# A pad behind the constants and one in the last stage: new byte places for the matmul operands of a hybrid S5 and pooling layer

## The chip, the cores and the metric

One core of one Trainium2 chip runs the whole kernel as one program. The metric is the device time of one execution in microseconds (us). Engines are named as in the profile: PE (matmuls), PEld (PE's weight loads, which run beside matmuls), DVE, ACT and POOL (elementwise work), SP (issues most DMAs).

## The reference, cut to what matters

One layer on `x` of shape (1, 2048, 1024), all in float32:

```python
h = rmsnorm(x, norm_g)
proj = h @ w_in + b_in                       # 1024 x 4096: ua, za, ub, zb (512 each), ga, gb (1024 each)
ya = s5_branch(ua, ...) * silu(za)           # diagonal complex state space, then a 512 x 512 GLU
yb = pool_branch(ub, pool_w, pool_scale) * silu(zb)
merged = sigmoid(ga) * (ya @ w_branch_a) + sigmoid(gb) * (yb @ w_branch_b)
x = x + merged @ w_out
return rmsnorm(x, final_norm_g)
```

## The kernel before, in words

**Matmuls.** Every large product is made from operands split into a high and a low part (`split`, L92 to 99), both kept as float32r tiles. `mm3` (L101 to 104) then issues three matmuls: the high weights against the high moving part (L102), the high weights against the low moving part (L103), the low weights against the high moving part (L104). In most stages the weights are 128 by 128 and the moving operand has 512 columns. Each matmul of the program brings its own weight load, so in a row of matmuls the weights of the next one are loaded while this one streams. "A group of three" below is one call of `mm3`.

**Stages, in the order of PE's work.** The sequence is cut into four chunks of 512 columns, and `hT0` to `hT3` hold the normalised, transposed input, 8 row blocks each.

- *Projections.* `proj_block` (L592) makes one block of 128 output channels for one chunk from 8 groups of three, moving operand `hT`, weights `wt` (or, for two of the four UA blocks, `w_first2` and `w_first3` from pool `d1`, which are kept for the whole UA stage, L189). The stages are UA, ZA (beside it `matrices`, which builds the state-space matrices on DVE and POOL, L424), UB and ZB with the pooling, and GA and GB. Beside the GA and GB blocks runs `scan` (L659), a generator that is advanced by one step per block: for each of 8 units it goes through `run_in`, `run_scan`, `table`, `run_taps`, the split of `sp` into `spl` (L830) and `run_out`, with matmuls of 256 columns.
- *GLU* (L1067 to 1086): moving operand `yhl`, weights `wg`, 64 groups of three.
- *Branches and output* (L1144 to 1196): for each chunk 64 groups with `yab` against `wt`, then 64 with `wo` against `mt`; the last row tile of the last chunk is cut into two halves of 256 columns.

**Order of the work.** The program is recorded in the order in which the code runs, for each engine one queue. `pump` (L131) splits the next weight tile and issues the load of one further on. Pools are opened and closed by stage. A tile that is laid over bytes of an earlier one waits for that one's last use, so where a tile lies decides what its first writer waits for.

**Places.** Pools `const`, `raw`, `w`, `stg`, `par` and the pools of the stages (`d1` to `d6`, `fin`) are laid one behind the other from the low end of a partition's memory. `hT`, `xp` and `big` (which holds `wo` and `yab`) are laid from the high end. The first pool is `const`:

```python
    RD = const.tile([128, G // 2], F32, name="RD")
    PH = const.tile([128, 2, G // 2], F32, name="PH")
```

Of the kernel before, what the change touches and what calls it, by code (L numbers as in the profile page):

```python
# [9 lines left out]
F32 = mybir.dt.float32  # L10
F32R = mybir.dt.float32r
# [25 lines left out]
def hybrid_kernel(ctx: ExitStack, tc: tile.TileContext, x, norm_g, w_in, b_in, log_dt, lam_re, lam_im,  # L37
# [9 lines left out]
    const = ctx.enter_context(tc.tile_pool(name="const", bufs=1))  # L47
# [7 lines left out]
    def sub(stack, name, side="left"):  # L55
        return stack.enter_context(tc.tile_pool(name=name, bufs=1, side=side, reuse_waits="tile"))
# [21 lines left out]
    rcnt = const.tile([128, 16], F32, name="rcnt")  # L78
    RD = const.tile([128, G // 2], F32, name="RD")
    PH = const.tile([128, 2, G // 2], F32, name="PH")  # L80

    def bcol(n):
        return cols[:, n:n + 1]
# [42 lines left out]
    hl = {}  # L126
# [58 lines left out]
    idn = par.tile([128, 128], F32, name="idn")  # L185
    s_d = ExitStack()
    d1 = sub(s_d, "d1")

    def w_first(key):  # L189
        t = d1.tile([128, 2, 1024], F32R, name=f"w_first{key[1]}")  # L190
        hl[key] = t
        return t[:, 0, :], t[:, 1, :], lambda r: r

    UA, ZA, UB, ZB, GA, GB = 0, 4, 8, 12, 16, 24
# [4 lines left out]
    for n in range(NB):  # L199
        w_in_job(n, plain if n < 2 else w_first)  # L200
# [10 lines left out]
    def ts(o, i, s1, o0, s2=None, o1=None):  # L211
        if s2 is None:
            V.tensor_scalar(out=o, in0=i, scalar1=s1, scalar2=None, op0=o0)
        else:
            V.tensor_scalar(out=o, in0=i, scalar1=s1, scalar2=s2, op0=o0, op1=o1)
# [6 lines left out]
    def pieces(v, bits, count):  # L222

        import struct
        if (v, bits, count) not in kept:
            res, left = [], v
            for _ in range(count - 1):
                m, e = math.frexp(left)
                q = math.ldexp(math.floor(m * 2 ** bits), e - bits)
                res.append(q)  # L230
                left -= q
            res.append(struct.unpack("f", struct.pack("f", left))[0])
            kept[v, bits, count] = res
        return kept[v, bits, count]
# [67 lines left out]
    def params(d, V, ldt, lam, dn):  # L302
# [61 lines left out]
        for h in range(2):  # L364
            r = slice(h * 64, (h + 1) * 64)
            V.tensor_copy(out=PH[r, 0], in_=ang[r, h::2])
        a0, a1, pn = PH[:, 0], PH[:, 1], d.tile([128, H], F32, name="pn")
        turn = pieces(64 * math.pi, 11, 4)
# [290 lines left out]
    def scan(d):  # L659
# [53 lines left out]
        def phases():  # L713
# [4 lines left out]
            for j in range(LV):  # L718
                ts(th[:, j], PH[:, 1], float(T << j), ALU.mult)
                ts(lo[:, j], PH[:, 0], float(T << j), ALU.mult)  # L720
            ts(n, th, 2.0 / math.pi, ALU.mult, MAGIC, ALU.add)
# [174 lines left out]
    for i in reversed(range(NB)):  # L896
# [23 lines left out]
        for k in range(2):  # L920
            n = min(T, win - 1 - k * T)
# [145 lines left out]
    for c in range(NCH):  # L1067
        t = yhl[c]
# [23 lines left out]
    d6 = sub(s_d, "d6")  # L1092
# [4 lines left out]
    def load_gate(c, n):  # L1097
        t = d6.tile([128, 2, 512], F32, tag="gt", bufs=3, name="gt")
        SP.dma_start(out=t, in_=Gd[n][c].rearrange("b p k -> p b k"))
        gts[c, n] = t  # L1100
# [22 lines left out]
    def finish(tt):  # L1123
# [12 lines left out]
            A.dma_start(out=outr[tt // 2, k0:k0 + 128, cs], in_=r[:, cs])  # L1136
        x2.pop(tt)

    load_gate(0, 0)
    load_gate(0, 1)  # L1140
    gb = d6.tile([128, D], F32, name="gb")
# [82 lines left out]
```

## Time and profile before

| | |
|---|---|
| median of 3 runs | 1236.32 us (1235.59 to 1238.8) |
| the profiled execution | 1238.27 us, of which the span of the profile 1236.4 us |
| PE busy | 1205.5 us (97% of the span), 5413 matmuls |
| weight loads busy | 975.1 us (79%) |
| DVE, ACT, POOL busy | 730.8, 395.3, 346.4 us |
| mean granted clock of TensorE | 0.993 of full |

The profile starts at the first instruction. The time of an execution is longer than the span by what lies around it, here 1.87 us. A matmul's duration in the profile reaches to a modelled end, and neighbours overlap; how fast PE goes is read from one matmul's start to the next one's.

### The profile page before, as it was taken

The page shows a single profiled execution, that of the slowest core. Times are in us where ns is not written, and L with a number is a line of the kernel's source. Part 1 is how long each engine was busy: PE and PEld are TensorE (multiplying, and loading weights), DVE is VectorE, ACT ScalarE, POOL GpSimd, SP SyncE. Part 2 cuts the span into 40 slices and gives each one's busy share as a digit, 9 for nine tenths or more (in the row PEclk, how much of TensorE's full clock was granted, in tenths as well). Part 3 has the DMA queues.
Part 4 walks back from the last instruction along what each step waited for, and adds up shares of the span by engine and source line. Part 5 has one row for each costly group of instructions (what it writes and reads, how often), then busy time and mean ns, then how long its engine had stood idle before and what let it go on. Part 6 is the DMA issues. An engine that isn't in the chain of part 4 may idle for free. (4 is left out here: it accounts for less than half of the span.)

```text
span 1236.4 us, 14778 instructions
## 1 busy us (share of the span) xinstructions
PE 1205.5 (97%) x5413; PEld 975.1 (79%) x5413; DVE 730.8 (59%) x1310; ACT 395.3 (32%) x622; POOL 346.4 (28%) x232
## 2 busy tenths in 40 slices
PE   6999989999999999999999999999999999999996
PEld 5887867788888888888888888887878888888885
DVE  5586378153543668777788773046565855755615
ACT  6542211222222232443333432244333322322202
POOL 3321167011110212332334321234562312213312
PEclk9999989999999999999999999999999999999998
DMA  8413233201111232433334332178766553563502
GB/s 295 133 43 84 58 112 126 80 17 54 43 45 43 83 110 88 129 91 110 113 94 128 96 102 78 66 227 253 247 218 209 182 188 131 175 207 105 188 1 102
DMA packets 149783, 149.94 MB, mean 121 GB/s; under 512 B 23584, under 2 KB 111184, under 8 KB 149712
## 3 DMA queue, kind: packets, MB, share of 16 engines
q1 hardware_dynamic: 127424, 112.28, 30.6%
q10 hardware_dynamic: 22288, 36.73, 7.9%
q8 instruction: 42, 0.69, 0.2%
q14 instruction: 29, 0.24, 0.1%
HBM read 99.43 MB, written 49.55 MB: 120 GB/s over the span
## 5 line engine op out<-in xcount | busy, mean ns | idle before, releaser
L102 PE MATMUL mm<-hT,wt 128*128 128x512 f32 x960 | 382.5, 398 | 0.0
L103 PE MATMUL mm<-hT,wt 128*128 128x512 f32 x960 | 380.6, 396 | 0.0
L104 PE MATMUL mm<-hT,wt 128*128 128x512 f32 x960 | 379.9, 396 | 0.0
L104 PEld LDWEIGHTS mm<-hT,wt 128*128 128x128 f32 x960 | 180.8, 188 | 44.1
L103 PEld LDWEIGHTS mm<-hT,wt 128*128 128x128 f32 x960 | 181.1, 189 | 43.5 <-DVE hT L98 0.9
L102 PEld LDWEIGHTS mm<-hT,wt 128*128 128x128 f32 x960 | 181.2, 189 | 42.7
L96 POOL TENSOR_TENSOR wt<-raw,wt 128x1024 fp32r<-128x1024 f32 x30 | 85.5, 2849 | 316.5 <-ACT wt L94 316.5
L1027 ACT ACTIVATE go<-mm,half 128x512 f32<-128x512 f32 x64 | 43.9, 686 | 204.9 <-PE mm L104 190.2
L102 PE MATMUL mm<-yab,wt 128*128 128x512 f32 x256 | 101.2, 395 | 1.8 <-DVE gt L1160 1.8
L104 PE MATMUL mm<-yab,wt 128*128 128x512 f32 x256 | 101.0, 395 | 0.0
L103 PE MATMUL mm<-yab,wt 128*128 128x512 f32 x256 | 101.0, 395 | 0.0
L94 ACT ACTIVATE wt<-raw 128x1024 fp32r<-128x1024 f32 x62 | 65.5, 1057 | 60.7 <-PE mm L104 34.2
L1162 POOL TENSOR_TENSOR m<-gt 128x512 f32<-128x512 f32 x32 | 52.1, 1630 | 100.4 <-DVE gt L1160 71.6
L1121 POOL TENSOR_TENSOR r<-r,gb 128x512 f32<-128x512 f32 (+1 forms) x33 | 41.1, 1260 | 138.4 <-ACT xt L1118 138.3
L96 DVE TENSOR_TENSOR wt<-raw,wt 128x1024 fp32r<-128x1024 f32 x32 | 58.6, 1831 | 19.7 <-ACT wt L94 19.6
L845 ACT ACTIVATE st<-mm,half 128x512 f32<-128x512 f32 x32 | 22.1, 690 | 145.9 <-PE mm L104 114.5
L1160 DVE SCALAR_TENSOR_TENSOR gt<-gt,mm 128x512 f32<-128x512 f32 x64 | 42.3, 680 | 32.8 <-PE mm L104 27.9
L102 PEld LDWEIGHTS mm<-yab,wt 128*128 128x128 f32 x256 | 48.0, 187 | 14.4 <-issue 2.6
L104 PEld LDWEIGHTS mm<-yab,wt 128*128 128x128 f32 x256 | 48.0, 187 | 11.7
L103 PEld LDWEIGHTS mm<-yab,wt 128*128 128x128 f32 x256 | 48.0, 187 | 11.6
L104 PE MATMUL mm<-wo,mt 128*128 128x512 f32 (+1 forms) x136 | 52.0, 383 | 0.0
L103 PE MATMUL mm<-wo,mt 128*128 128x512 f32 (+1 forms) x136 | 52.0, 382 | 0.0
(272 smaller groups left out, 1920.3 us busy)
## 6 DMA issues: line engine op xcount, KB each, us to landing
xt<-in_x SPq DMA_DIRECT2D x32, 512.0 KB, 5.4
raw<-in_w_in SPq DMA_DIRECT2D x32, 512.0 KB, 4.4
Gd<-go ACTq DMA_DIRECT2D x64, 256.0 KB, 2.4
gt<-Gd SPq DMA_DIRECT2D x32, 512.0 KB, 4.8
raw<-in_w_branch_a SPq DMA_DIRECT2D x32, 256.0 KB, 3.1
raw<-in_w_branch_b SPq DMA_DIRECT2D x32, 256.0 KB, 3.5
out<-r ACTq DMA_DIRECT2D x32, 256.0 KB, 2.3
Ud<-uo ACTq DMA_DIRECT2D x16, 256.0 KB, 2.1
```

Of the source, the lines that this page charges most:

```text
L94: A.activation(hi, src, AF.Copy, scale=1.0 if scale is None else scale)
L96: (eng or V).tensor_tensor(out=lo, in0=src, in1=hi.bitcast(F32), op=ALU.subtract)
L102: PE.matmul(ps, lhsT=sh, rhs=mh, start=first, stop=False)
L103: PE.matmul(ps, lhsT=sh, rhs=ml, start=False, stop=False)
L104: PE.matmul(ps, lhsT=sl, rhs=mh, start=False, stop=last)
L845: A.activation(t, ps, AF.Tanh, bias=hcol(n), scale=0.5)
L1027: A.activation(o, ps, AF.Tanh, bias=hcol(n), scale=0.5)
L1121: GP.tensor_tensor(out=r, in0=r, in1=gb[:, cs], op=ALU.mult)
L1160: V.scalar_tensor_tensor(out=gt[:, b], in0=gt[:, b], scalar=1.0, in1=pss[b], op0=ALU.add, op1=ALU.mult)
L1162: GP.tensor_tensor(out=m, in0=gt[:, 0], in1=gt[:, 1], op=ALU.add)
```

## The change

A tile of 48 floats (192 bytes per partition) that nothing uses is added at the end of `const`, and one of 32 floats (128 bytes) as the first tile of `d6`. The two `w_first` tiles are allocated when `d1` is opened, ahead of all its other tiles. No instruction is added, removed or moved on any engine.

```diff
@@ -78,6 +78,7 @@
     rcnt = const.tile([128, 16], F32, name="rcnt")
     RD = const.tile([128, G // 2], F32, name="RD")
     PH = const.tile([128, 2, G // 2], F32, name="PH")
+    const.tile([128, 48], F32, name="lpad")
 
     def bcol(n):
         return cols[:, n:n + 1]
@@ -185,10 +186,10 @@
     idn = par.tile([128, 128], F32, name="idn")
     s_d = ExitStack()
     d1 = sub(s_d, "d1")
+    firsts = {n: d1.tile([128, 2, 1024], F32R, name=f"w_first{n}") for n in (2, 3)}
 
     def w_first(key):
-        t = d1.tile([128, 2, 1024], F32R, name=f"w_first{key[1]}")
-        hl[key] = t
+        t = hl[key] = firsts[key[1]]
         return t[:, 0, :], t[:, 1, :], lambda r: r
 
     UA, ZA, UB, ZB, GA, GB = 0, 4, 8, 12, 16, 24
@@ -1136,6 +1137,7 @@
             A.dma_start(out=outr[tt // 2, k0:k0 + 128, cs], in_=r[:, cs])
         x2.pop(tt)
 
+    d6.tile([128, 32], F32, name="pad6")
     load_gate(0, 0)
     load_gate(0, 1)
     gb = d6.tile([128, D], F32, name="gb")
```

What this does to the places, as the allocator gives them (start of the operand, in bytes modulo 512; every slice of these tiles that a matmul reads starts a multiple of 512 bytes further on):

| moving operand, weights | columns | groups of three | before: moving / weights | now: moving / weights |
|---|---|---|---|---|
| `hT`, `wt` | 512 | 960 | 480 / 288 | 480 / 480 |
| `hT`, `w_first2`, `w_first3` | 512 | 64 | 480 / 192 and 256 | 480 / 32 |
| `yab`, `wt` | 512 | 256 | 480 / 288 | 480 / 480 |
| `wo`, `mt` | 512 | 248 | 480 / 160 | 480 / 480 |
| `wo`, `mt` | 256 | 16 | 480 / 160 | 480 / 480 |
| `yhl`, `wg` | 512 | 64 | 288 / 288 | 480 / 480 |
| `plhl`, `pw` (pooling) | 512 | 16 | 384 / 384 | 64 / 64 |
| `uu`, `bt`; `uu`, `mz`; `spl`, `ca` (scan) | 256 | 96 | 288 / 288 | 480 / 480 |

Some tiles lie over other bytes than before, so a few first writers wait for something else. The queue of SP at the loads of `matrices` is one such place (`cn`, and `B_1320` and `B_1321`, now `B_1321` and `B_1322`, hold the matrices C and B in pool `d2`). Before:

```order
L427 DMA cn<-in_ssm_c_re 128x4x64 [waits DMAHW1_49,PE_49]
L427 DMA cn<-in_ssm_c_im 128x4x64 [waits DMAHW3_49]
L427 DMA cn<-in_ssm_c_re 128x4x64 [waits DMAHW4_49]
L431 DMA B_1320<-in_ssm_b_re 64x32x16 [waits DMAHW5_49]
L432 DMA B_1320<-in_ssm_b_im 64x32x16 [waits DMAHW6_49]
```

The same place on SP's queue in the changed kernel:

```order
L428 DMA cn<-in_ssm_c_re 128x4x64 [waits DMAHW1_49,PE_49]
L428 DMA cn<-in_ssm_c_im 128x4x64 [waits DMAHW3_49]
L428 DMA cn<-in_ssm_c_re 128x4x64 [waits DMAHW4_49]
L432 DMA B_1321<-in_ssm_b_re 64x32x16 [waits DMAHW5_49,PE_49]
L433 DMA B_1321<-in_ssm_b_im 64x32x16 [waits DMAHW6_49]
```

The order is the same; the first load of B now also waits for PE, since it is laid over `w_first3`, whose last matmul ends the UA stage.

## Rows read from the trace of the kernel before

**Rows 1.** The page: PE's busy time, share and instructions; its granted clock in 40 slices.
```profile
PE 1205.5 (97%) x5413; PEld 975.1 (79%) x5413; DVE 730.8 (59%) x1310; ACT 395.3 (32%) x622; POOL 346.4 (28%) x232
...
PEclk9999989999999999999999999999999999999998
```

**Rows 2.** Groups by form on PE: shapes, xcount | busy us, mean ns | idle before.
```profile
L102 PE MATMUL mm<-hT,wt 128*128 128x512 f32 x960 | 382.5, 398 | 0.0
...
L102 PE MATMUL mm<-yab,wt 128*128 128x512 f32 x256 | 101.2, 395 | 1.8 <-DVE gt L1160 1.8
...
L102 PE MATMUL pso<-wo,mt 128*128 128x512 f32 x128 | 50.6, 395 | 0.0
...
L102 PE MATMUL mm<-wo,mt 128*128 128x512 f32 x120 | 47.4, 395 | 0.0
```

**Rows 3.** Timeline of PE and its weight loads, ZA stage: start us, us, engine.
```profile
155.45 0.39 PE L102 MATMUL mm<-hT,wt 128*128 128x512 f32 x1
155.45 0.19 PEld L103 LDWEIGHTS mm<-hT,wt 128*128 128x128 f32 x1
```

**Rows 4.** Timeline of PE, 21 groups on hT, then 13 groups on wo.
```profile
587.86 0.39 PE L102 MATMUL mm<-hT,wt 128*128 128x512 f32 x1
...
602.56 0.39 PE L102 MATMUL mm<-hT,wt 128*128 128x512 f32 x1
...
1205.66 0.40 PE L102 MATMUL mm<-wo,mt 128*128 128x512 f32 x1
...
1214.76 0.40 PE L102 MATMUL mm<-wo,mt 128*128 128x512 f32 x1
```

**Rows 5.** Timeline of PE, 27 groups of the GLU stage.
```profile
822.15 0.39 PE L102 MATMUL mm<-yhl,wg 128*128 128x512 f32 x1
...
840.51 0.39 PE L102 MATMUL mm<-yhl,wg 128*128 128x512 f32 x1
```

**Rows 6.** Timeline of PE, 51 groups on wo in the third chunk.
```profile
1097.22 0.39 PE L102 MATMUL pso<-wo,mt 128*128 128x512 f32 x1
...
1132.24 0.39 PE L102 MATMUL mm<-wo,mt 128*128 128x512 f32 x1
```

**Rows 7.** Timeline of PE, 256 columns: 4 groups of the scan, 15 on wo.
```profile
535.17 0.28 PE L102 MATMUL psx<-uu,bt 128*128 128x256 f32 x1
...
536.61 0.40 PE L102 MATMUL mm<-hT,wt 128*128 128x512 f32 x1
...
1220.36 0.28 PE L102 MATMUL mm<-wo,mt 128*128 128x256 f32 x1
...
1225.67 0.28 PE L102 MATMUL mm<-wo,mt 128*128 128x256 f32 x1
```

**Rows 8.** PE's waits: engine, tile and line <- releaser: us, times, longest.
```profile
PE psb L505 <- DVE bp L218: 5.6, 3, 3.8
PE mm L102 <- DVE gt L1160: 1.8, 2, 1.2
...
PE psT L561 <- DVE hT L98: 1.6, 1, 1.6
```

**Rows 9.** Timeline of DVE and PE in the scan's second unit.
```profile
502.29 1.39 DVE L785 TENSOR_TENSOR z<-z,psy 128x512 f32<-128x512 f32 x2 [7.44 <-POOL z L782]
...
532.50 1.22 DVE L96 TENSOR_TENSOR spl<-sp,spl 128x1024 fp32r<-128x1024 f32 x1
...
533.36 0.28 PE L102 MATMUL psy<-spl,ca 128*128 128x256 f32 x1
533.77 0.39 PE L103 MATMUL psy<-spl,ca 128*128 128x256 f32 x1
```

**Rows 10.** SP's first load of B; last matmuls on w_first; B's first use on DVE.
```profile
120.34 0.93 SPq L431 DMA_DIRECT2D B<-in_ssm_b_re  x1
...
L104 PE MATMUL mm<-hT,w_first x64: 392/395/398, 30.9 to 123.5; 128*128 128x512 f32 x64
...
L215 DVE TENSOR_SCALAR B<-B,sgn x1: 478/478/478, 149.2 to 149.2; 128x512 f32<-128x512 f32 x1
```

## The prediction

> **What bounds the kernel now.** I read the page first, then PE's groups by form, then single starts on PE's timeline, then the waits. The page says that PE is busy 97% of the span and that its clock is granted almost throughout [rows 1]. Nearly all of that is matmuls with 512 columns: 960 groups of three on `hT` and `wt`, 256 on `yab`, 128 and 120 on `wo` [rows 2], so 1464 groups. In the long stretches no engine makes PE wait; the waits that the profile ascribes to other engines after the start are a few microseconds in all [rows 8]. So the time is the number of matmuls times the distance between their starts, and a change of that distance by one nanosecond is worth 1464 x 3 x 1 ns = 4.4 us.
>
> That distance is what this change can touch. On `hT` 21 groups take 602.56 - 587.86 = 14.70 us, so 0.700 us for a group and 233 ns for a matmul; 13 groups on `wo` in the last chunk take 9.10 us, again 0.700 [rows 4]. The clock there is at the upper of its two levels, 2.4 GHz [rows 1], so it is not the clock that can give more. What runs beside each matmul is the weight load of the next one: it starts at the same instant as the matmul [rows 3]. The two read different tiles of the same memory, and the places of those tiles are what is changed.
>
> The trace holds one stage that already has its operands as the change puts all others: in the GLU stage moving operand and weights both start at 288 modulo 512. There 27 groups take 840.51 - 822.15 = 18.36 us, 0.680 for a group and 226.7 ns for a matmul [rows 5]. Shape, type, clock and number of loads are those of the other stages. That is the argument for a gain: 20 ns a group where the two places agree.
>
> **A rule against it.** The Trainium skill, "TensorE: Matmul & The Clock Gate", section "Step-by-step: what each phase is for", says that TensorE reads the moving operand and the weights through two independent ports, so that loading the next weights takes nothing from the running matmul. By that rule places would be free and the sum zero. The page's own distance for 512 columns is about 216 ns; neither 233 nor 227 is that, and two stages that differ in no count differ by 20 ns a group, so I weigh the rows above the rule but keep its outcome as a rival.
>
> **The change part by part.** Nothing is added to or taken from any engine's queue; only distances and a few waits can change.
>
> 1. *`hT` with `wt`*: 960 groups go from unequal to equal places. 960 x 20 ns = 19.2 us less.
> 2. *`yab` with `wt`*: 256 x 20 ns = 5.1 us less.
> 3. *`wo` with `mt`, 512 columns*: 248 groups. In the third chunk these already go faster: 51 groups take 35.02 us, 0.687 a group [rows 6], at the same places as in the last chunk. So the 64 of that chunk gain 7 ns each (0.4 us) and the other 184 gain 20 (3.7 us): 4.1 us less.
> 4. *`wo` with `mt`, 256 columns*: 15 groups take 5.31 us, 0.354 each, at unequal places; the scan's groups, at equal places, take 1.44 / 4 = 0.360 [rows 7]. 16 x 6 ns = 0.1 us more.
> 5. *`w_first`*: 64 groups stay unequal (32 against 480, a difference no row shows). Bounds: nothing, or the 20 ns, 1.3 us. I take nothing, since every unequal pair with 512 columns that I read stands near 0.700.
> 6. *GLU, scan, pooling*: equal before and after, so nothing. That 480 does what 288 does is assumed; it is rival A below.
> 7. *The new wait of B's load*: the load would be issued after the UA stage's last matmul, 123.5 us instead of 120.34, and DVE first touches B at 149.2 [rows 10]. Three microseconds out of more than twenty cost nothing. Queued behind it are only the other three loads of B, and the next weight load comes much later.
>
> Sum of the gross gain: 19.2 + 5.1 + 4.1 - 0.1 = 28.3 us.
>
> Not all of it stays, because in four places PE is already waiting or nearly so, and what it gains before such a place it waits longer there.
>
> - *Scan.* In the second unit DVE works without a gap from 502.29 until the split of `spl` ends at 532.50 + 1.22 = 533.72, and the second matmul on it starts at 533.77, 410 ns behind the first instead of 120: PE waits 0.3 us already [rows 9]. A unit has 6 blocks, 48 groups, so PE would come 0.96 us earlier, of which the start of DVE's run follows by one block (0.16). About 0.8 to 0.9 us are lost in such a unit; the same wait stands in three of the eight (the second, the fourth and the sixth); in the others the split is done before PE comes. 3 x 0.87 = 2.6 us.
> - *`matrices`.* PE waits 5.6 us for DVE's `bp` before transposes [rows 8]. About 64 groups lie between the start of chunk 3 and there: up to 1.3 us are lost. DVE's steps there are partly called up by PE's blocks and come earlier too, so I take 1.0.
> - *UA stage.* PE waits 1.6 us for the split of `hT` [rows 8]; 48 faster groups lie before it, so 1.0 us.
> - *First branch chunk.* There two weight splits per tile are asked for, and PE waits 1.8 us for DVE [rows 8]. 64 groups: 1.3 us, all lost.
>
> Together 5.9 us (bounds: nothing, and twice that if more units of the scan become tight). Net: 28.3 - 5.9 = 22.4 us. The profiled execution took 1238.27 us, which is 1.95 above the median of the three runs. 1238.27 - 22.4 = 1215.9, against the median 1213.9; I say **1214 us**. This case's own range: with nothing given back and `w_first` faster too, 1236.3 - 29.6 = 1206.7; with 11.8 given back, 1236.3 - 16.5 = 1219.8.
>
> **The rivals.**
>
> *A. Nothing moves.* The GLU stage may be faster because its moving operand is at 288, or for its place low in memory, and not because the two agree; or, as the rule above has it, places do not matter and the GLU stage differs for another reason. For it: the 0.687 of one chunk on `wo` shows that the distance can change with the places unchanged. Against it: the GLU stage is the one that is at 0.680, and no stretch that I read elsewhere is. Then the 64 GLU groups may lose their 20 ns, 1.3 us: 1236 to 1238 us.
>
> *B. Half of it.* The distance depends also on how loads and matmuls fall against each other, and the rhythm that sets in is the 0.687 one. Then 960 + 256 + 184 = 1400 groups gain 13 ns, 18.2 us, of which about 4 are given back: 1222 us.
>
> *C. Slower: equal places collide.* With 256 columns the equal pair is the slower one, 0.360 against 0.354 [rows 7]: two reads that begin at the same place at the same instant may hinder each other, and with 512 columns at 480 that could hold too. It decides if 480 behaves unlike 288. Priced with the row: 1464 x 7 ns = 10 us more, 1246 us. Against it: in the GLU stage with 512 columns equal is faster.
>
> *D. The change doesn't do what it says.* For `w_first` it does not: 32 is not 480. That is only 64 groups, and the pooling's 16 pairs are at 64 but equal. It moves no more than 1.3 us and has no chance of its own.
>
> **How the numbers follow.** Forecast 0.60, A 0.18, B 0.13, C 0.09. The range from 1206 to 1237 holds the forecast's own (1207 to 1220), B and most of A. A measurement of this kernel can tell about 0.3% from no change, 3.7 us: forecast and B lie beyond it on the fast side, A within it, C on the slow side. So faster 0.73, same 0.18, slower 0.09.
>
> **What would show it.** On PE's timeline the groups on `hT` and `yab` should stand 0.680 us apart, their mean duration some 7 ns below that of now [rows 2], while the GLU stage keeps 0.680 and `w_first` stays near 0.700. In the scan PE's waits for `spl` should grow to about 1.2 us in every second unit. If `hT` stays at 0.700 and GLU rises to it, A is right; 0.687 throughout is B; over 0.700 is C. If the distances fall to 0.680 and the time still does not, the step on what is given back is wrong, and PE's waits would show where.

## The result, and the profile after

| | before | changed |
|---|---|---|
| median of the runs on one chip | 1236.33 us (1235.59 to 1238.8, 4 runs) | 1216.88 us (1216.27 to 1217.42, 4 runs) |
| the profiled execution | 1238.27 us, span 1236.4 us | 1217.19 us, span 1215.4 us |
| mean granted clock | 0.993 | 0.994 |

The changed kernel takes 0.9839 of the time before (95% interval 0.9822 to 0.9856): 19.5 us less, where 22.4 was predicted and 1214 us stood on record. The same kernel timed once more, beside the experiments, gave 0.9846 (0.9833 to 0.9859).

The page of the changed kernel, PE's busy time and its granted clock, against [rows 1]:

```profile
PE 1179.0 (97%) x5413; PEld 974.8 (80%) x5413; DVE 730.3 (60%) x1310; ACT 395.2 (33%) x622; POOL 345.6 (28%) x232
...
PEclk9999999999999999999999999999999999999998
```

The same instructions, the same clock; PE is busy 26.5 us less, and no other engine's time moved by more than a microsecond. The groups by form on PE (x count | busy us, mean ns | idle before) show where, against [rows 2]; lines have moved down by one in the code:

```profile
L103 PE MATMUL mm<-hT,wt 128*128 128x512 f32 x960 | 377.1, 393 | 0.0
...
L103 PE MATMUL mm<-yab,wt 128*128 128x512 f32 x256 | 100.1, 391 | 3.3 <-DVE gt L1162 3.3
...
L103 PE MATMUL pso<-wo,mt 128*128 128x512 f32 x128 | 49.8, 389 | 0.0
...
L103 PE MATMUL mm<-wo,mt 128*128 128x512 f32 x120 | 46.7, 389 | 0.0
```

The mean duration (the last number before the second bar) fell by 4 to 6 ns. The distance itself is in the starts. PE's timeline of the changed kernel (start us, us, engine, line): 21 groups on `hT`, 27 of the GLU stage, 12 on `yab`, 51 on `wo` in the third chunk, 13 in the last:

```profile
577.50 0.39 PE L103 MATMUL mm<-hT,wt 128*128 128x512 f32 x1
...
591.78 0.39 PE L103 MATMUL mm<-hT,wt 128*128 128x512 f32 x1
...
804.32 0.39 PE L103 MATMUL mm<-yhl,wg 128*128 128x512 f32 x1
...
822.68 0.39 PE L103 MATMUL mm<-yhl,wg 128*128 128x512 f32 x1
...
978.00 0.39 PE L103 MATMUL mm<-yab,wt 128*128 128x512 f32 x1
...
986.16 0.39 PE L103 MATMUL mm<-yab,wt 128*128 128x512 f32 x1
...
1077.96 0.39 PE L103 MATMUL pso<-wo,mt 128*128 128x512 f32 x1
...
1112.64 0.39 PE L103 MATMUL mm<-wo,mt 128*128 128x512 f32 x1
...
1186.08 0.39 PE L103 MATMUL mm<-wo,mt 128*128 128x512 f32 x1
...
1194.92 0.39 PE L103 MATMUL mm<-wo,mt 128*128 128x512 f32 x1
```

14.28 / 21, 18.36 / 27, 8.16 / 12, 34.68 / 51 and 8.84 / 13 are all 0.680 us: the distance that only the GLU stage had before [rows 5] now stands in all five, where [rows 4] had 0.700 and [rows 6] 0.687. Two places did not gain. From the same timeline, 6 groups on `w_first` and 15 on `wo` with 256 columns:

```profile
64.05 0.40 PE L103 MATMUL mm<-hT,w_first 128*128 128x512 f32 x1
...
68.25 0.40 PE L103 MATMUL mm<-hT,w_first 128*128 128x512 f32 x1
...
1199.00 0.28 PE L103 MATMUL mm<-wo,mt 128*128 128x256 f32 x1
...
1204.39 0.28 PE L103 MATMUL mm<-wo,mt 128*128 128x256 f32 x1
```

`w_first`, the pair that is still unequal, stays at 4.20 / 6 = 0.700, and the 256-column groups went from 0.354 [rows 7] to 5.39 / 15 = 0.359.

PE's waits in the changed kernel (tile and line <- releaser: us, times, longest), against [rows 8]:

```profile
PE psb L506 <- DVE bp L219: 6.2, 3, 3.9
PE mm L103 <- DVE gt L1162: 3.3, 3, 1.4
PE psy L104 <- DVE spl L97: 3.1, 3, 1.0
PE mm L103 <- ACT yhl L95: 2.2, 1, 2.2
PE psT L562 <- DVE hT L99: 1.6, 1, 1.6
```

The waits for `spl` are new in the list, those for `gt` grew from 1.8 us, those for `bp` from 5.6, and the one for `hT` stayed. The scan's second unit, now PE and DVE of the changed kernel, against [rows 9]:

```profile
522.62 0.28 PE L103 MATMUL psy<-spl,ca 128*128 128x256 f32 x1
523.92 0.39 PE L104 MATMUL psy<-spl,ca 128*128 128x256 f32 x1 [1.03 <-DVE spl L97]
...
496.52 3.30 DVE L749 TENSOR_TENSOR xs<-xs,tab 128x1024 f32<-128x1024 f32 x1
...
522.65 1.22 DVE L97 TENSOR_TENSOR spl<-sp,spl 128x1024 fp32r<-128x1024 f32 x1
```

The second matmul on `spl` starts 1.30 us behind the first, before it was 0.41. The same gap stands at 597.89 and 673.19: the second, fourth and sixth unit.

### The profile page after: what moved, and what is told of

Read it like the earlier page. It is cut to its first block, busy times and chain, and to the rows that moved or that the text cites. A ratio compares the mean times of both kernels' runs of the same rounds, so it can differ in the third digit from the quotient of the medians.

```text
span 1215.4 us, 14777 instructions
## 1 busy us (share of the span) xinstructions
PE 1179.0 (97%) x5413; PEld 974.8 (80%) x5413; DVE 730.3 (60%) x1310; ACT 395.2 (33%) x622; POOL 345.6 (28%) x232
## 5 line engine op out<-in xcount | busy, mean ns | idle before, releaser
L103 PE MATMUL mm<-hT,wt 128*128 128x512 f32 x960 | 377.1, 393 | 0.0
L104 PE MATMUL mm<-hT,wt 128*128 128x512 f32 x960 | 375.6, 391 | 0.2 <-DVE hT L99 0.2
L105 PE MATMUL mm<-hT,wt 128*128 128x512 f32 x960 | 374.8, 390 | 0.0
L103 PE MATMUL mm<-yab,wt 128*128 128x512 f32 x256 | 100.1, 391 | 3.3 <-DVE gt L1162 3.3
L104 PE MATMUL mm<-yab,wt 128*128 128x512 f32 x256 | 99.7, 390 | 0.0
L105 PE MATMUL mm<-yab,wt 128*128 128x512 f32 x256 | 99.7, 389 | 0.0
L1162 DVE SCALAR_TENSOR_TENSOR gt<-gt,mm 128x512 f32<-128x512 f32 x64 | 42.2, 680 | 28.3 <-PE mm L105 23.6
```

Of the source, the lines that this page charges most:

```text
L103: PE.matmul(ps, lhsT=sh, rhs=mh, start=first, stop=False)
L104: PE.matmul(ps, lhsT=sh, rhs=ml, start=False, stop=False)
L105: PE.matmul(ps, lhsT=sl, rhs=mh, start=False, stop=last)
L1162: V.scalar_tensor_tensor(out=gt[:, b], in0=gt[:, b], scalar=1.0, in1=pss[b], op0=ALU.add, op1=ALU.mult)
```

## The experiments

### The constants' pad alone

Only the 192 bytes behind `const` are added; `mt` then lies 128 bytes below `wo`, and the two `w_first` tiles at 384 and 448.

```diff
     PH = const.tile([128, 2, G // 2], F32, name="PH")
+    const.tile([128, 48], F32, name="lpad")
```

> The pad behind the constants alone: wt goes to 480 (equal to hT and yab), mt to 352 (128 below wo), w_first to 384 and 448. Theory E (equal places modulo 512 of the moving operand and of the weights loaded beside it make the 0.680 us group): hT and yab groups 0.680, wo groups and w_first near 0.700 (0.687 possible on wo, as once before). Time: the whole change less 248 x 20 ns = 5 us on wo, so about 1222 us. Rival P (the period is 128 bytes, not 512): wo groups at 0.680 too, time as the whole change, 1217 us.

Measured: 1219.02 us (1218.66 to 1221.48, 4 runs), 0.9862 of before (0.9839 to 0.9885). `hT` and `yab` are at 0.680 as in the changed kernel, `w_first` at 0.700. PE's timeline, 30 groups on `wo` with `mt` 128 bytes below:

```profile
1163.78 0.39 PE L103 MATMUL pso<-wo,mt 128*128 128x512 f32 x1
...
1184.70 0.40 PE L103 MATMUL mm<-wo,mt 128*128 128x512 f32 x1
```

20.92 / 30 = 0.697: a difference of 128 bytes gains almost nothing, so theory E holds here and rival P does not. This one pad makes most of the gain. The second pad is worth 17 ns on each of 248 groups, 4.2 us by the starts; by the two ratios it is about 3 us, with intervals that overlap, and the spans of the two profiles (1216.8 and 1215.4 us) differ by 1.4. Theory E's 1222 us is 3 too many. In this execution PE's waits for `gt` were 0.5 us, 2.8 less than in the changed kernel's. Those waits vary between executions of the same kernel (3.3 and 1.6 us in the two of the changed one), so whether the second pad lengthens them, and gives back part of its gain there, is not settled.

### Four distances in one kernel

The kernel before, with 64 bytes laid beside each of `hT1` to `hT3`. The weights stay at 288; `hT0` to `hT3` start at 480, 416, 352 and 288.

```diff
-        hT[c] = sub(s_hT[c], f"hTp{c}", "right").tile([128, 2, NK, 512], F32R, name=f"hT{c}")
+        pool = sub(s_hT[c], f"hTp{c}", "right")
+        hT[c] = pool.tile([128, 2, NK, 512], F32R, name=f"hT{c}")
+        if c:
+            pool.tile([128, 16], F32, name=f"rpad{c}")
```

> The kernel before, with 64 bytes behind each of hT1, hT2 and hT3, so that hT0 to hT3 stand at 480, 416, 352 and 288 while wt stays at 288: weights 192, 128, 64 and 0 below the moving operand in one run. Theory E: groups on hT3 at 0.680, those on hT0, hT1 and hT2 near 0.700. Rival Q (weights at 480 are what is fast, whatever the moving operand): none at 0.680. Rival P (period 128): hT1 and hT3 at 0.680. Rival S (period 64): all at 0.680 except that before none was, so S is nearly out. Time by E: 240 groups x 20 ns = 4.8 us less than before, about 1231 to 1232 us.

Measured: 1231.39 us (one run), as theory E had it. PE's timeline, the starts of four blocks of 8 groups one after the other, on `hT0`, `hT1`, `hT2` and `hT3`; then 16 groups on `hT3`, cut behind the fourth:

```profile
233.19 0.39 PE L102 MATMUL mm<-hT,wt 128*128 128x512 f32 x1
...
238.79 0.39 PE L102 MATMUL mm<-hT,wt 128*128 128x512 f32 x1
...
244.36 0.40 PE L102 MATMUL mm<-hT,wt 128*128 128x512 f32 x1
...
249.86 0.40 PE L102 MATMUL mm<-hT,wt 128*128 128x512 f32 x1
...
255.35 0.39 PE L102 MATMUL mm<-hT,wt 128*128 128x512 f32 x1
...
785.42 0.40 PE L102 MATMUL mm<-hT,wt 128*128 128x512 f32 x1
...
788.19 0.39 PE L102 MATMUL mm<-hT,wt 128*128 128x512 f32 x1
...
796.35 0.40 PE L102 MATMUL mm<-hT,wt 128*128 128x512 f32 x1
```

`hT0` 5.60 / 8 = 0.700, `hT1` 5.57 / 8 = 0.696, `hT2` 5.50 / 8 = 0.687, and `hT3`, the equal pair, 0.680 over the 12 groups from 788.19 on (8.16 us). Just behind another buffer it is slower, 2.77 / 4 = 0.692 there and 5.49 / 8 = 0.686 in the first stretch. With the weights at 288 the gain is had at 288; in the changed kernel, with the weights at 480, the same `hT` has it at 480. So it is neither the one place nor the other that counts, but the two operands' relation. Not foreseen were the 0.687 of `hT2`, 64 below the weights, and what carries over from the buffer ahead: over all unstalled groups (those that no wait interrupts) the means are 700.2, 697.8, 688.8 and 685.2 ns, the medians 700, 696, 687 and 681.

### Weights half of 512 bytes away

The kernel before, with `rcnt` (64 bytes) moved out of `const` to behind the staging pool. Of the matmul operands only the weights move, from 288 to 224: 256 below `hT` and `yab`, equal if 256 is the period and unequal if it is 512.

```diff
+    late = ctx.enter_context(tc.tile_pool(name="late", bufs=1))
+    rcnt = late.tile([128, 16], F32, name="rcnt")
...
-    rcnt = const.tile([128, 16], F32, name="rcnt")
```

> The kernel before, with the table rcnt (64 bytes) moved behind stg, so that the wt tiles of the ring stand at 224, 256 below hT and yab; every other tile stays where it was. Theory E: hT and yab groups near 0.700, time as before, 1236 us. Rival R (period 256): 0.680 on hT and on the two thirds of yab whose weights come from the ring, time near 1215 to 1220 us.

Measured: 1221.44 us (one run), 14.5 less than the median of the kernel before in the same session, 1235.92. Groups on `hT` are at 0.680. On `yab` both values stand side by side, since the weights come from two pools there, one at 224 (173 groups, median 680 ns) and one still at 288 (79 groups, median 702). PE's timeline, 7 groups of the first kind, 6 of the second:

```profile
859.21 0.39 PE L103 MATMUL mm<-yab,wt 128*128 128x512 f32 x1
...
863.97 0.39 PE L103 MATMUL mm<-yab,wt 128*128 128x512 f32 x1
...
865.35 0.39 PE L103 MATMUL mm<-yab,wt 128*128 128x512 f32 x1
...
869.55 0.39 PE L103 MATMUL mm<-yab,wt 128*128 128x512 f32 x1
```

4.76 / 7 = 0.680 and 4.20 / 6 = 0.700. The distances are those of rival R, and theory E as it stood is wrong: what must agree is the place modulo 256, not modulo 512 as the change has it. The time is 1.4 us above R's range.

### Near, but not equal

A pad of 160 bytes puts the weights at 448: equal to `hT1` to `hT3`, which are moved to 448 too, and 32 below `hT0` and `yab`. `mt` lies at 320.

```diff
+    const.tile([128, 40], F32, name="lpad")
...
+        if c == 1:
+            pool.tile([128, 8], F32, name=f"rpad{c}")
```

> The kernel before with 160 bytes behind the constants, and 32 bytes behind hT1: wt at 448, hT0 and yab at 480 (weights 32 below), hT1, hT2 and hT3 at 448 (equal), mt at 320 (160 below wo). Theory E in its strict form: hT1 to hT3 at 0.680, hT0 and yab near 0.700. Rival N (near is enough): hT0 and yab at 0.680 as well. Rival Q (480 itself): none at 0.680. Time by E: 720 x 20 ns = 14 us less before what is given back, about 1223 to 1225 us.

Measured: 1227.23 us (one run), 2 us above what theory E gave. PE's timeline, three blocks of 8 groups, on `hT0`, `hT1` and `hT2`:

```profile
231.43 0.40 PE L103 MATMUL mm<-hT,wt 128*128 128x512 f32 x1
...
237.03 0.40 PE L103 MATMUL mm<-hT,wt 128*128 128x512 f32 x1
...
242.51 0.39 PE L103 MATMUL mm<-hT,wt 128*128 128x512 f32 x1
...
247.95 0.39 PE L103 MATMUL mm<-hT,wt 128*128 128x512 f32 x1
```

0.700, 0.685 (the first groups behind `hT0` are slower), 0.680. Thirty-two bytes apart is as slow as any other distance; nearness is worth nothing. `wo`, 160 above `mt`, got slower than before: a mean of 702.6 ns against 696.6, which over its 248 groups is 1.5 of the 2 us.

The runs together, for 512 columns, by weights minus moving modulo 256 (median ns of a group):

| 0 | 32 | 64 | 96 | 128 | 160 | 192 | 224 |
|---|---|---|---|---|---|---|---|
| 680 | 698 to 699 | 700 to 702 | 702 | 695 to 697 | 700 | 687, sometimes 700 | 699 to 700 |

[Rows 6] belong to the column 192: before, `wo` and `mt` stood 192 apart, the one distance at which both 687 and 700 occur. In this kernel and in the one with four distances, too, pairs 192 apart ran at 687.

One pair does not fit the column 0: the pooling's 16 groups, whose operands stand at equal places in every kernel here, have a median of 698 ns before and of 704 in the changed kernel. They come singly or in twos between blocks on `hT`. Two in a row in the changed kernel, on PE's timeline:

```profile
409.11 0.40 PE L103 MATMUL psp<-plhl,pw 128*128 128x512 f32 x1
...
409.81 0.39 PE L103 MATMUL psp<-plhl,pw 128*128 128x512 f32 x1
```

From its start to the next one's the first takes 0.70 us; the second takes 0.687, and the three groups on `hT` behind them 0.698, 0.691 and 0.692, before 0.680 is back. So in these runs equal places give 0.680 only where some groups on the same operands follow each other.

### Only the low weights unequal

The changed kernel, with the GLU stage's low weights 64 bytes further on: its high weights at 480, its low ones at 32, the moving operand at 480 in chunks 0 and 2 and at 32 in chunks 1 and 3. It asks which of a matmul's neighbours must agree: the weights it uses, or those loaded beside it for the next one.

```diff
...
-                    wg = d5.tile([128, 2, NB, 512], F32R, name="wg")
+                    wgt = d5.tile([128, 2 * NB * 512 + 16], F32R, name="wg")
+                    wg = [wgt[:, o:o + NB * 512].rearrange("p (k n) -> p k n", k=NB) for o in (0, NB * 512 + 16)]
...
```

> The changed kernel with 64 bytes between the high and the low weights of wg, so that in the GLU stage the high ones stand at 480 and the low ones at 32; the moving operand stands at 480 in chunks 0 and 2 and at 32 in chunks 1 and 3. Theory L (what counts is the moving operand against the weights that are loaded while it streams, those of the next matmul): in chunks 0 and 2 the second matmul (which streams while the low weights are loaded) is followed later, by about 233 ns, the first and third by about 227; in chunks 1 and 3 the other way round, the first and third by about 233. Rival U (what counts are the weights in use): in chunks 0 and 2 the third is the long one, in chunks 1 and 3 the short one. The three may share out a difference among them, then only the sum of a group tells: about 687 in chunks 0 and 2 and 693 to 700 in chunks 1 and 3 by both. Time: within 1 us of the changed kernel.

Measured: 1218.93 us (one run). PE's timeline, 7 groups of chunk 0, then 6 of chunk 1:

```profile
809.69 0.39 PE L103 MATMUL mm<-yhl,wg 128*128 128x512 f32 x1
...
814.54 0.39 PE L103 MATMUL mm<-yhl,wg 128*128 128x512 f32 x1
...
824.22 0.39 PE L103 MATMUL mm<-yhl,wg 128*128 128x512 f32 x1
...
828.34 0.39 PE L103 MATMUL mm<-yhl,wg 128*128 128x512 f32 x1
```

4.85 / 7 = 0.693 and 4.12 / 6 = 0.687; the expectation had the sums the other way round, about 687 and 693 to 700. In chunks 0 and 2 one matmul in three is unequal, 64 apart modulo 256, and costs 13 ns of the 20; in chunks 1 and 3 two are, but 192 apart, the distance that has 687 elsewhere as well, so these say little. Averaged over the groups of chunks 0 and 2, the three distances are 228.3, 228.9 and 236.0 ns; of chunks 1 and 3, 230.8, 230.1 and 228.4. The long one in the first case is behind the matmul that uses the unequal weights, not beside their load. That fits the use; but if the slowing shows one matmul late, it fits the load as well, and this order can't tell the two apart. It stays open.

### The scan's wait taken away

The changed kernel, timed again in the same session: 1218.82 us (1216.4 to 1219.36, 4 runs), 0.9846 of before.

> The changed kernel once more, as the measure for the two beside it on the same chip: 1217 us by every theory, PE waiting about 1.2 us for the split of sp in three units of the scan.

Then the same with one weight split per round of four blocks recorded a block earlier while the scan runs:

```diff
+            if c == 2 and idx < 12:
+                pump()
...
-        pump()
+        if idx >= 12:
+            pump()
```

> The changed kernel with the weight split of a GA or GB tile asked for after the third block of the tile before instead of after its fourth, for the first twelve of the sixteen tiles. Theory G (what the scan gives back is given back because in every second unit two of POOL's wt splits, which read two tiles, hold up two-input operations of DVE by 2 us each, and PE then waits for spl): the split that began at 495.5 us moves into DVE's pause before L786, that DVE operation takes 1.2 us instead of 3.3, PE's waits for spl go from 3.1 us in all to under 1 us, and the time falls by 2 to 3 us against the changed kernel, to about 1214 to 1215 us. Rival H (DVE's own work fills the unit, wherever POOL's splits lie): the waits stay at 3 us, or move to other units, and the time stays at 1217 us.

Measured: 1213.34 us (1211.92 to 1216.84, 4 runs), 0.981 of before (0.9794 to 0.9826). The timeline of POOL and DVE in the changed kernel's own profile shows what the move is about:

```profile
495.53 3.20 POOL L97 TENSOR_TENSOR wt<-raw,wt 128x1024 fp32r<-128x1024 f32 x1 [2.42 <-ACT wt L95]
```

and, with the split moved, POOL, DVE and PE:

```profile
489.49 2.40 POOL L97 TENSOR_TENSOR wt<-raw,wt 128x1024 fp32r<-128x1024 f32 x1 [14.46 <-ACT wt L95]
...
499.07 1.23 DVE L749 TENSOR_TENSOR xs<-xs,tab 128x1024 f32<-128x1024 f32 x1
...
525.15 0.28 PE L103 MATMUL psy<-spl,ca 128*128 128x256 f32 x1
525.27 0.28 PE L104 MATMUL psy<-spl,ca 128*128 128x256 f32 x1
```

In the changed kernel POOL's split runs from 495.53 to 498.73, and DVE's operation beside it takes 3.30 us (above), ending 1.1 us behind POOL's; alone it takes 1.23. The Trainium skill, "SBUF — State Buffer", section "SBUF: two separate sides", says that a DVE operation with two inputs in that memory and a GpSimd operation that reads there exclude each other, and that the one that starts first holds the other up for its whole instruction; the trace agrees, since 1.1 us is about what is left to do for an operation that waited until the split's end. With the split in DVE's pause, PE's two matmuls stand 0.12 us apart, and the waits for `spl`, 3.0 us in all in the run just above, leave the list. The two profiled executions differ by 2.5 us (1219.36 and 1216.84), about what these waits say. The medians differ by 5.5, more than that; the rest is not explained.

### Both: `w_first` equal as well

The kernel above, with 448 bytes ahead of `w_first`, so that both its tiles start at 480:

```diff
+    d1.tile([128, 112], F32, name="dpad")
     firsts = {n: d1.tile([128, 2, 1024], F32R, name=f"w_first{n}") for n in (2, 3)}
```

> The moved weight split of the run before and 448 bytes ahead of the w_first tiles, which puts them at 480 too. By theory E the 64 groups on w_first go from 0.700 to 0.680 us, 1.3 us less than without; if PE then waits longer at the start of the last UA chunk, up to 1 us of it is given back there. By G and E together 1213 to 1214 us; by H and E 1216 us.

Measured: 1212.09 us (1211.2 to 1213.41, 5 runs), 0.9796 of before (0.9782 to 0.9809): the fastest kernel here. PE's timeline, 5 groups on `w_first`:

```profile
66.46 0.39 PE L103 MATMUL mm<-hT,w_first 128*128 128x512 f32 x1
...
69.86 0.39 PE L103 MATMUL mm<-hT,w_first 128*128 128x512 f32 x1
```

3.40 / 5 = 0.680, so the 64 groups gain 1.3 us; the medians differ by 1.25, within the runs' spread.

## Why the prediction was right, and where it was off

The mechanism held: the forecast's case came, not nothing (A), not the half rhythm (B), not a collision (C). The second experiment and the changed kernel decide it together: within one kernel the four pieces of `hT` have four distances, where before all four stood at 700 ns, and `hT` at 480 is slow beside weights at 288 and fast beside weights at 480. They also decide against what the forecast drew from the rule against it, that places are free. The Trainium skill, "TensorE: Matmul & The Clock Gate", section "Step-by-step: what each phase is for", has loads and streaming on independent ports, the load taking nothing from the running matmul; the trace doesn't agree: 227 ns where the operands agree modulo 256 bytes, 233 to 234 at five of the other seven distances, at the same clock and with the same number of loads.

One step was wrong though the sum was not: the prediction took agreement modulo 512 as the condition, from the GLU stage [rows 5], where operands agree modulo both. The third experiment shows modulo 256. The change satisfies the stricter condition, so the time does not depend on it; 64 bytes less in `const` would have done for `hT`. Two readings of the rows were too smooth as well. The step on `w_first` says that every unequal pair stood near 0.700, while [rows 6] are an unequal pair at 0.687. And the GLU stage was not the only one with equal places and 512 columns: the pooling had them too, at 384, and its groups stood at 0.698. That spoke for rival A and was not weighed.

The terms, from the starts of all unstalled groups in the two profiles:

| term | predicted us | measured us |
|---|---|---|
| `hT`, 960 groups | -19.2 | -17.9 (700.0 to 681.4 ns) |
| `yab`, 256 | -5.1 | -5.0 (699.9 to 680.5) |
| `wo`, 248 | -4.1 | -4.1 (696.6 to 680.0) |
| `wo`, 256 columns | +0.1 | +0.1 (353.5 to 359.4) |
| `w_first` | 0 | 0 |
| scan's 256 columns, GLU | 0 | +0.1 |
| scan's waits | +2.6 | +2.7 (three of 0.89) |
| `matrices` | +1.0 | +0.7 |
| UA stage | +1.0 | -0.1 |
| first branch chunk | +1.3 | +0.4 |
| second branch chunk, GLU's waits, one wait at 73.4 | 0 | +1.1, +0.9, +0.4 |
| start, and matmuls at the lower clock | 0 | -0.5, -0.8 |
| net | -22.4 | -22.0; the spans differ by 21.0 |

The measured terms leave 1.0 us of the spans' difference unassigned. *Gross gain, items 1 to 6: 28.3 predicted, 26.8 found.* The term off is `hT`: the median is 680, the mean 681.4, because the groups behind another operand or a wait take 690 to 698 ns until the rhythm is back; the groups behind the pooling and those behind the scan make up about half a microsecond each. That `w_first` gained nothing was right, but modulo 256 it is no new distance: it stands 64 apart now, as `hT` and `wt` did before. Item 4, the loss with 256 columns, came out to the nanosecond; the groups on `spl`, equal before and now, took 2 ns longer (354.6 to 357.0), for which no cause was looked for.

*Item 7, B's load.* It was issued at 122.97 us instead of 120.34, and B was first used at 147.7: the cost is nothing, as said.

*What is given back.* The sum 5.9 came close to what the waits grew by, 6.1, but only the scan's share was right in itself; that the sums agree is luck. There the reasoning was complete: DVE's run was followed to its end, and PE's earlier arrival set against it. In the UA stage the wait did not grow: the gap behind the last matmul ahead of the transposes is 1.96 us, it was 2.03. The step counted on 48 faster groups ahead of it; the groups just ahead, those on `w_first`, are not among them. Whether DVE came earlier by as much as PE was not traced, so why nothing was lost stays open. The first branch chunk lost 0.4 instead of 1.3, and the second chunk, which had not waited before, lost 1.1 at 952.70 for the same `gt`. Even these two are of one execution: in the second profile of the changed kernel PE waited 1.6 us for `gt` in all, less than the 1.8 before, so it is not shown that the branch chunks give anything back. The GLU stage's waits for `yhl` (one of 1.7 us before, which [rows 8] leave out) grew by 0.9; the prediction had looked at its distance only and not at its waits. *The start and the lower clock:* in the spells of matmuls 427 ns apart behind the long waits near 100 and 172 us (granted clock 0.5, 1.2 GHz; both kernels have them), fewer matmuls fell into the second, which with the start gave 1.3 us back.

*The absolute number.* The profiled execution of before stood 1.95 us above its median, and the prediction took off as much; that of after stands 0.31 above its own. These 1.6 us and the 1.3 by which the profiled gain fell short of 22.4 are the 3 us between 1213.9 and 1216.9.

## What to carry to other kernels

Where weight loads run beside matmuls of 512 columns in float32r and PE is never idle, read the distance between starts stage by stage: two stages with the same shapes and different distances are a reason to look at where their operands lie. Here a pad that brought both operands to the same place modulo 256 bytes was worth 3% of each matmul, with no instruction changed. Then look where PE already waits, or nearly, since there the gain is handed back: in this kernel 3 of 27 us at three places of the scan, which moving one split by one block recovered.

## What was not expected of the hardware

- Equality is needed modulo 256, not 512 (680 ns with the weights at 224 and the moving operand at 480), and in steps of 32 bytes there is no gradient: 699 at 32 and 700 at 224. Only 192 (687) and 128 (695 to 697) lie between. Finer steps were not tried.
- At a difference of 192 the same code runs at 687 in one stretch and at 700 in another; what selects the rhythm was not found.
- With 256 columns the best of the four distances that occur is another: 353.5 ns a group at 192, 356 at 96, 360 at 0 and at 128.
- Behind other operands an equal pair needs two to four groups at 0.684 to 0.698 before it comes to 0.680, also where the operands ahead were at equal places themselves.
- Whether the weights in use or the next ones being loaded must agree is open, and why the distance matters at all no run here shows.
